# Per-head normalisation of the retention output: squares summed with tokens on partitions, factors spread on ScalarE and turned by four 128x128 transposes

## The chip, the cores and the metric

The kernel runs on one core of a Trainium2 chip. Its time is the device time of one execution in microseconds (us). Three executions of the kernel before took 1422.23, 1422.47 and 1424.04 us, with a median of 1422.47 us. A further execution was profiled; it took 1422.08 us. The profile names the engines PE (TensorE matmuls), PEld (TensorE weight loads), DVE (VectorE), ACT (ScalarE), POOL (GpSimd) and SP (SyncE, which issues the transfers here).

## The reference

Two layers of a hybrid backbone work on 1024 latent tokens and 256 context tokens of width 1024. In each layer one input projection feeds a short convolution, a two-directional retention with 6 heads of 64 channels, and a neighbourhood attention with 6 heads; each branch is gated, and one output projection with a LayerNorm closes the layer. The second layer needs no context output. The change concerns only the normalisation of the retention output, per token and head, over the head's 64 channels:

```
def head_norm(o):
    of = o.astype(F32)
    mu = jnp.mean(of, axis=-1, keepdims=True)
    var = jnp.mean(jnp.square(of - mu), axis=-1, keepdims=True)
    return (of - mu) * lax.rsqrt(var + LN_EPS)

y = from_heads(head_norm(o)) * jax.nn.silu(g)
```

In the kernel the mean is already removed when the values V are written (each head's V has its mean over channels subtracted), so what is left is a sum of squares, a reciprocal square root and a product.

## The kernel before, in words

Activations are kept transposed, channels on the 128 partitions and tokens along the free dimension. Tokens are cut in three groups: 512, 512 and 256 (context), numbered 0, 1 and 2. A projection unit (`proj_T`, lines 271 to 280) multiplies 128 columns of the weight with one token group in 24 matmuls: 8 chunks of the width, three products each of a high and a low part. Such matmuls, written to `ps_pj`, move 512 columns (256 for the context). `proj_V` (line 392) makes values with tokens on partitions: 24 matmuls of 256 columns for 128 tokens, in ten tiles. The weights come in 512-wide tiles through a ring of five (`wh`, the high part, cast on ACT at line 225; `wl`, the low part, subtracted on DVE or POOL at line 217). A value unit holds four of the five.

The six heads are three pairs p = 0, 1, 2; a pair fills 128 partitions. For each pair the program first runs the K, Q and V projections and then starts `core(p)` (line 420), a generator: it gives up control with `yield n` and is resumed when the recorded cost of the matmuls issued since has reached n. The next pair's projections (for p = 2 the gate projections of line 620) are issued meanwhile, so the yields set the PE order, which is taken as written. The other engines' orders come from a scheduler. Every engine works its own list in order.

Inside `core`, after the chunk states, each token group goes through `output` (lines 516 to 533: PE accumulates `ps_pv`, ACT copies it to `oT` and squares it into `ret_sq`), `scores` of the next group (PE, then DVE and POOL make `ret_s` and `ret_q`), and `norm` (lines 535 to 571). Layer 0 takes the groups in the order 2, 0, 1 for each pair, layer 1 takes 0 and 1: 9 and 6 norms, 15 in all, 12 of them of 512 tokens (four chunks of 128) and 3 of 256 (two chunks). The last norm of a pair is followed on PE by projection matmuls, the others by the next group's `output`.

The norm before has eight steps: a PE product of the 0/1 selector `selv` with the squares, chunk j on partitions 32j to 32j+31 (line 541); a 32x32-block transpose on DVE to `ct` (544); scale and add of epsilon to `c8` on POOL (546); the power -1/2 to `r8` on POOL (550); a split of the factor into a high and a low part, `rr`, in three DVE operations (554 to 556); after a yield, a PE transpose of `rr` (559) and a masked spread to `r16` on DVE (561); after another yield, one PE product with `sel16` that brings the factors to all channels (566); and the product with `oT` on DVE (569). The PSUM tag `pt` has two banks, and `norm` takes three in turn.

Of the kernel before, what the change touches and what calls it, by code (L numbers as in the profile page):

```python
# [10 lines left out]
F = mybir.dt.float32  # L11
R = mybir.dt.float32r
AF = mybir.ActivationFunctionType
ALU = mybir.AluOpType
# [6 lines left out]
HD = 64  # L21
ALPHA = (2 * DEPTH) ** 0.25
EPS = 1e-5
# [10 lines left out]
def f32(ap):  # L34
    return ap.bitcast(F)
# [43 lines left out]
def backbone(ctx: ExitStack, tc: tile.TileContext, io):  # L79
    nc = tc.nc  # L80
    pe, act, dve, pool, sp = nc.tensor, nc.scalar, nc.vector, nc.gpsimd, nc.sync
    od = Order()

    def mm(out, lhsT, rhs, start, stop, cost):
        pe.matmul(out, lhsT, rhs, start=start, stop=stop)  # L85
        od.t += cost
        od.poll()

    const = ctx.enter_context(tc.tile_pool(name="const", bufs=1))
# [5 lines left out]
    def bank(tag, bufs):  # L95
        return psum.tile([128, 512], F, tag=tag, bufs=bufs, name=f"ps_{tag}")
# [3 lines left out]
    ps_t = lambda: bank("pt", 2)  # L100
    ps_v = lambda: bank("pv", 1)

    def load_const(name, shape):
        t = const.tile(shape, F, name=f"c_{name}")
        sp.dma_start(t, io[name])
        return t
# [5 lines left out]
    mhalf = const.tile([128, 8], F, name="mhalf")  # L112
# [12 lines left out]
    def transpose(out, in_):  # L125
        pe.transpose(out, in_, ident[:in_.shape[0], :in_.shape[0]])  # L126
        od.t += 109
        od.poll()
# [124 lines left out]
    def new_h():  # L253
        return [[hpool.tile([128, KC, n], R, tag=f"h{j}{g}", name=f"h{j}{g}")
                 for j in range(2)] + [[]] for g, (o, n) in enumerate(GRP)]
# [7 lines left out]
    def accumulate(ps, w, h, g, kks):  # L263
        n = GRP[g][1]
        ready(h, g)
        for kk in kks:
            for i, (a, b) in enumerate(PASS):
                mm(ps[:, :n], w(kk, a), h[g][b][:, kk, :], kk == 0 and i == 0,
                   kk == KC - 1 and i == 2, n / 2.37)
# [113 lines left out]
    def retention(l, h, yT, vn, ctx_q, begin):  # L383
        groups = (0, 1, 2)
        qgroups = groups if ctx_q else (0, 1)
        with ExitStack() as st:
            rp = st.enter_context(tc.tile_pool(name=f"ret{l}", bufs=2, reuse_waits="tile"))
# [32 lines left out]
            def core(p, kT, qT, V, oT):  # L420
# [95 lines left out]
                def output(g, sq_in):  # L516
                    o, n = GRP[g]
                    ov = ps_v()
                    for j in range(n // 128):
                        c = o // 128 + j  # L520
                        for step in range(2):
                            for hh in range(2):
                                dst = ov[hh * 64:hh * 64 + 64, j * 128:(j + 1) * 128]
                                if step == 0:
                                    mm(dst, V[:, c, hh * HD:(hh + 1) * HD],
                                       sq_in[hh][0][:, j * 128:(j + 1) * 128], True, False, 141)
                                else:
                                    mm(dst, SS[:, c, hh * HD:(hh + 1) * HD],
                                       sq_in[hh][1][:, j * 128:(j + 1) * 128], False, True, 141)
                    act.copy(oT[:, o:o + n], ov[:, :n])  # L530
                    sq = t2("ret_sq")
                    act.activation(sq[:, :n], oT[:, o:o + n], AF.Square)
                    return sq

                def norm(g, sq):
                    o, n = GRP[g]
                    nch = n // 128
                    vps = ps_t()
                    np_ = 32 * nch
                    for j in range(nch):  # L540
                        mm(vps[32 * j:32 * j + 32, :128], selv, sq[:, j * 128:(j + 1) * 128],
                           True, True, 80)
                    ct = rp.tile([128, 128], F, tag="ct", bufs=1, name="ct")
                    dve.transpose(ct[:np_], vps[:np_, :128])
                    c8 = rp.tile([128, 4, 2], F, tag="c8", bufs=2, name="c8")
                    pool.tensor_scalar(
                        c8[:np_], ct[:np_].rearrange("p (b c) -> p b c", c=32)[:, :, 0:2],
                        1.0 / HD, EPS, ALU.mult, ALU.add)
                    r8 = rp.tile([128, 4, 2], F, tag="r8", bufs=2, name="r8")
                    pool.tensor_tensor(r8[:np_], c8[:np_], mhalf[:np_, 0:8].rearrange(  # L550
                        "p (b c) -> p b c", c=2), ALU.pow)
                    rr = rp.tile([128, 4, 2, 2], F, tag="rr", bufs=2, name="rr")
                    rh = rp.tile([128, 4, 2], R, tag="rh", bufs=2, name="rh")
                    dve.tensor_copy(rh[:np_], r8[:np_])
                    dve.tensor_copy(rr[:np_, :, 0, :], f32(rh[:np_]))
                    dve.tensor_tensor(rr[:np_, :, 1, :], r8[:np_], f32(rh[:np_]), ALU.subtract)
                    yield 6500
                    rt = ps_t()
                    transpose(rt[0:16, :np_], rr[:np_].rearrange("p b x h -> p (b x h)"))
                    r16 = rp.tile([16, 4, 128], R, tag="r16", bufs=1, name="r16")  # L560
                    dve.tensor_tensor(r16[:, :, :np_],
                                      rt[0:16, :np_].unsqueeze(1).to_broadcast([16, 4, np_]),
                                      mask16.unsqueeze(2).to_broadcast([16, 4, np_]), ALU.mult)
                    yield 2700
                    bc = ps_t()
                    mm(bc[:, :n].rearrange("p (b q) -> p b q", b=4), sel16,
                       r16[:, :, :np_], True, True, n / 2.37)
                    ov_v = oT[:, o:o + n].rearrange("p (g b t) -> p b g t", b=4, t=32)
                    dve.tensor_tensor(ov_v, ov_v,
                                      bc[:, :n].rearrange("p (b g t) -> p b g t", b=4, t=32),  # L570
                                      ALU.mult)

                order = ((2,) if ctx_q else ()) + (0, 1)
                sc = scores(order[0])
# [3 lines left out]
                for i, g in enumerate(order):  # L578
                    sq = output(g, sc)
                    yield 800  # L580
                    if i + 1 < len(order):
                        sc = scores(order[i + 1])
                    yield 800
                    yield from norm(g, sq)
                    done.append((p, g))

            tiles = []
            for p in range(3):
# [4 lines left out]
                    oT=rp.tile([128, TOK], F, tag="oT", bufs=3, name="oT")))  # L593
# [319 lines left out]
    h = new_h()  # L913
# [51 lines left out]
    def first_w(u):  # L965
        return lambda kk, i: wts[u][kk // 4][i][:, (kk % 4) * 128:(kk % 4 + 1) * 128]
# [5 lines left out]
    def begin_stage(i):  # L972
        kks = STAGES[i]
        tiles = stage_load(kks)
        if i == 0:
            small()
        stage_x(kks)
        if 0 in kks or 4 in kks:
            for u, c0 in enumerate((C_RK, C_RQ)):
                wts[u].append(w_half(0, c0, kks[-1] // 4))  # L980
        return od.start(stage(kks, tiles))

    begin_stage(0)
    for i, kks in enumerate(STAGES):
        if i + 1 < len(STAGES):
            begin_stage(i + 1)
        if i == 1:
            selv = load_const("selv", [128, 32])
            mask16 = load_const("mask16", [16, 4])
            sel16f = load_const("sel16", [16, 128])  # L990
            sel16 = const.tile([16, 128], R, name="sel16r")
            dve.tensor_copy(sel16, sel16f)
            rmask = load_const("rmask", [128, 16])
            cmask = load_const("cmask", [128, 24])
        for g in range(3):
            od.until(lambda: all((g, kk) in have for kk in kks))
            accumulate(acc_k[g], first_w(0), h, g, kks)
            if g < 2:
                accumulate(acc_q[g], first_w(1), h, g, kks)
# [26 lines left out]
    for l in range(DEPTH):  # L1026
# [12 lines left out]
        with ExitStack() as st:  # L1039
# [62 lines left out]
            for t in range(8 if last else 10):  # L1102
# [16 lines left out]
                for c in range(DM // w):  # L1119
                    hf, o = c * w // 512, c * w % 512  # L1120
# [32 lines left out]
            if not last:  # L1153
                h, mod = h_next, mod_n
# [88 lines left out]
```

## Time and profile before

| what | value |
|---|---|
| three executions, median | 1422.47 us |
| profiled execution, its own time | 1422.08 us |
| its span (first to last instruction) | 1420.3 us |
| granted TensorE clock over the span | 0.993 |
| busy: PE / DVE / ACT / POOL | 1371.0 / 959.7 / 469.0 / 330.1 us |
| norms, first and last `oT` product | 131.0 and 1029.4 us |

Times in the views are counted from the span's start. A row of the timeline gives the start, the time from the first start to the last end of what is merged in it, the engine, the line, the operation, the tiles written and read, the shapes and the count; in brackets stands the idle time before it and what ended it. Neighbouring matmuls overlap, so what a step on PE costs is read from starts, not from durations. An fp32 matmul leaves two records in the trace, a projection matmul one. A row of waits gives the total, the number and the longest.

### The profile page before, as it was taken

The numbers are of one execution on the slowest core, as the hardware profiler recorded it, in microseconds if no ns is written. First come the engines' busy times: TensorE is split into PE (matmuls) and PEld (weight loads), VectorE is DVE, ScalarE is ACT, GpSimd is POOL, SyncE is SP. The second block draws the span as 40 slices with busy tenths as digits, with TensorE's granted clock in tenths as the row PEclk, the third lists the DMA queues.
The fourth block names the chain that finished last, engine by engine and source line by source line (L and its number), as shares of the span: only waits on it lengthen the run. The fifth ranks groups of instructions, "written<-read, shape, count | busy, mean of one in ns | idle before, by whom it ended". The sixth has DMA issues, their size and how long they took to land.

```text
span 1420.3 us, 23906 instructions
## 1 busy us (share of the span) xinstructions
PE 1371.0 (97%) x9016; PEld 1156.0 (81%) x9016; DVE 959.7 (68%) x2392; ACT 469.0 (33%) x985; POOL 330.1 (23%) x281
## 2 busy tenths in 40 slices
PE   7999999999999999999999999999999999999997
PEld 4788878877888888878887798888777878787886
DVE  4677465648887886865887656565578756365686
ACT  3322121223452443443344322121234435354310
POOL 1405132342002203000344405050431031120121
PEclk9999999999999999999999999999999999999999
DMA  9720110224124224116443211111242220302642
GB/s 282 224 57 20 38 38 28 70 72 125 54 60 141 74 69 122 50 56 204 152 139 107 81 49 31 49 30 50 75 138 67 59 73 30 93 23 83 203 153 89
DMA packets 160852, 126.33 MB, mean 89 GB/s; under 512 B 10320, under 2 KB 146144, under 8 KB 160736
## 3 DMA queue, kind: packets, MB, share of 16 engines
q1 hardware_dynamic: 160736, 124.80, 28.8%
q8 instruction: 71, 1.16, 0.3%
q14 instruction: 45, 0.37, 0.1%
HBM read 103.01 MB, written 21.76 MB: 88 GB/s over the span
## 4 chain that ended last, share of the span: by engine, by line
PE 80%; DVE 9%; issue 2%; DMA 1%; POOL 1%; ACT 1%; SPq 0%; POOLq 0%; DVEq 0%; ACTq 0%
PE ps_pj L85 62%; PE ps_pv L85 6%; PE ps_pt L126 6%; PE ps_s L85 6%; DVE acc L197 1%; DVE rsw L379 1%; DMA E<-in_rpb 1%; PE ps_pt L85 1%; POOL B L711 1%; DVE P L692 1%; DVE ret_q L508 0%; DVE qd L487 0%; DVE wl L217 0%; DVE ret_s L499 0%; DVE sm L406 0%
## 5 line engine op out<-in xcount | busy, mean ns | idle before, releaser
L85 PE MATMUL ps_pj<-h,wh 128*128 128x512 f32 (+1 forms) x2128 | 622.8, 373 | 3.2 <-ACT wh L225 3.2
L85 PEld LDWEIGHTS ps_pj<-h,wh 128*128 128x128 f32 x2128 | 379.3, 189 | 67.0 <-issue 5.5
L85 PE MATMUL ps_pj<-h,wl 128*128 128x512 f32 (+1 forms) x1064 | 397.1, 373 | 0.0
L85 PEld LDWEIGHTS ps_pj<-h,wl 128*128 128x128 f32 x1064 | 201.4, 189 | 34.3 <-issue 4.0
L85 PE MATMUL ps_pj<-wo,yh 128*128 128x512 f32 (+1 forms) x608 | 181.7, 381 | 0.0
L85 PE MATMUL ps_pj<-wh,h 128*128 128x256 f32 x960 | 180.4, 288 | 0.7 <-ACT nv L412 0.7
L85 PEld LDWEIGHTS ps_pj<-wh,h 128*128 128x128 f32 x960 | 153.7, 196 | 2.8 <-issue 1.8
L217 POOL TENSOR_TENSOR wl<-wr,wh 128x512 fp32r<-128x512 f32 x32 | 43.8, 1369 | 461.0 <-ACT wh L225 386.3
L85 PE MATMUL ps_pj<-wl,h 128*128 128x256 f32 x480 | 138.2, 288 | 4.4 <-DVE wl L217 2.9
L85 PEld LDWEIGHTS ps_pj<-wo,yh 128*128 128x128 f32 x608 | 111.9, 188 | 21.2 <-issue 0.5
L85 PE MATMUL ps_pj<-wo,yl 128*128 128x512 f32 (+1 forms) x304 | 116.1, 382 | 0.0
L225 ACT CAST wh<-wr 128x512 fp32r<-128x512 f32 x128 | 79.2, 621 | 111.1 <-PE ps_pj L85 100.1
L197 DVE SCALAR_TENSOR_TENSOR acc<-wm,c_silu,acc 128x256 f32<-128x256 f32 x224 | 110.5, 534 | 5.7 <-DMA wm<-in_w_mod 5.2
L751 ACT ACTIVATE P<-P,nm 128x640 f32<-128x640 f32 (+1 forms) x96 | 77.2, 804 | 96.9 <-DVE nm L749 96.0
L85 PEld LDWEIGHTS ps_pj<-wl,h 128*128 128x128 f32 x480 | 94.0, 196 | 5.3 <-DVE wl L217 3.1
L761 ACT COPY PT<-ps_pt 128x512 f32<-128x512 f32 (+1 forms) x108 | 60.5, 560 | 87.9 <-PE ps_pt L126 87.0
L217 DVE TENSOR_TENSOR wl<-wr,wh 128x512 fp32r<-128x512 f32 x96 | 68.5, 716 | 29.1 <-ACT wh L225 27.0
L126 PE MATMUL ps_pt<-c_ident,P 128*128 128x128 f32 x480 | 73.1, 279 | 3.2 <-DVE P L692 2.9
L85 PE MATMUL ps_s<-KS,QH 128*128 128x256 f32 x204 | 59.7, 311 | 9.3 <-DVE mx L747 7.6
L85 PEld LDWEIGHTS ps_pj<-wo,yl 128*128 128x128 f32 x304 | 57.2, 188 | 10.8 <-issue 0.5
L126 PEld LDWEIGHTS ps_pt<-c_ident,P 128*128 128x128 f32 x480 | 54.5, 141 | 13.9 <-issue 7.4
L85 PE MATMUL ps_pv<-PT,VA 128*64 128x128 f32 x960 | 64.3, 278 | 0.0
(175 smaller groups left out, 1951.7 us busy)
## 6 DMA issues: line engine op xcount, KB each, us to landing
wr<-in_w_in SPq DMA_DIRECT2D x104, 256.0 KB
wm<-in_w_mod SPq DMA_DIRECT2D x128, 128.0 KB
wr<-yT SPq DMA_DIRECT2D x36, 256.0 KB
yT<-ystage SPq DMA_DIRECT2D x32, 256.0 KB
wr<-in_w_out SPq DMA_DIRECT2D x32, 256.0 KB
wm<-in_w_mod SPq DMA_DIRECT2D x12, 512.0 KB
wr<-in_w_in SPq DMA_DIRECT2D x48, 128.0 KB
z<-in_x SPq DMA_DIRECT2D x8, 512.0 KB
```

What stands on the lines that cost most here:

```text
L85: pe.matmul(out, lhsT, rhs, start=start, stop=stop)
L126: pe.transpose(out, in_, ident[:in_.shape[0], :in_.shape[0]])
L197: dve.scalar_tensor_tensor(acc[:, v], t, c, acc[:, v], ALU.mult, ALU.add)
L217: eng.tensor_tensor(lo, raw, f32(hi), ALU.subtract)
L225: act.copy(hi, raw)
L379: dve.tensor_tensor(sw, sw, rs[:, o:o + n], ALU.mult)
L692: dve.tensor_scalar(P[:, :n], P[:, :n], r, 0.5, ALU.mult, ALU.mult)
L711: pool.tensor_tensor(B, bass.AP(tensor=E.tensor, offset=E[:, o:o + 1].offset, ap=[list(E.ap[0]), [1, nc_], [RPB_W, 16]]), rmask.unsqueeze( ...
L751: act.activation(P[:, :256 + n], P[:, :256 + n], AF.Exp, bias=nm, accum_out=s)
L761: act.copy(PT[:, :n], pt[:, :n])
```

## The change

The squares become the stationary operand: for each chunk of 128 tokens PE multiplies the transposed squares by `selv`, now two columns wide, which leaves the two sums of a token on the token's partition. DVE scales them and adds epsilon straight from PSUM, POOL takes the power as before, ACT repeats each factor over 64 columns (`rb`, 128x512) with the scale 0.5, and after one yield PE transposes `rb` in four plain 128x128 transposes. DVE multiplies `oT` by the result. The DVE transpose, the high and low parts, the masked spread, the `sel16` product and the constants `mask16` and `sel16` go. One yield of 6000 stands where 6500 and 2700 stood.

```diff
@@ norm(g, sq)
                     vps = ps_t()
-                    np_ = 32 * nch
                     for j in range(nch):
-                        mm(vps[32 * j:32 * j + 32, :128], selv, sq[:, j * 128:(j + 1) * 128],
-                           True, True, 80)
-                    ct = rp.tile([128, 128], F, tag="ct", bufs=1, name="ct")
-                    dve.transpose(ct[:np_], vps[:np_, :128])
+                        mm(vps[:, 2 * j:2 * j + 2], sq[:, j * 128:(j + 1) * 128], selv,
+                           True, True, 220)
                     c8 = rp.tile([128, 4, 2], F, tag="c8", bufs=2, name="c8")
-                    pool.tensor_scalar(
-                        c8[:np_], ct[:np_].rearrange("p (b c) -> p b c", c=32)[:, :, 0:2],
-                        1.0 / HD, EPS, ALU.mult, ALU.add)
+                    dve.tensor_scalar(c8[:, :nch], vps[:, :2 * nch].rearrange(
+                        "p (b c) -> p b c", c=2), 1.0 / HD, EPS, ALU.mult, ALU.add)
                     r8 = rp.tile([128, 4, 2], F, tag="r8", bufs=2, name="r8")
-                    pool.tensor_tensor(r8[:np_], c8[:np_], mhalf[:np_, 0:8].rearrange(
-                        "p (b c) -> p b c", c=2), ALU.pow)
-                    rr = rp.tile([128, 4, 2, 2], F, tag="rr", bufs=2, name="rr")
-                    rh = rp.tile([128, 4, 2], R, tag="rh", bufs=2, name="rh")
-                    dve.tensor_copy(rh[:np_], r8[:np_])
-                    dve.tensor_copy(rr[:np_, :, 0, :], f32(rh[:np_]))
-                    dve.tensor_tensor(rr[:np_, :, 1, :], r8[:np_], f32(rh[:np_]), ALU.subtract)
-                    yield 6500
-                    rt = ps_t()
-                    transpose(rt[0:16, :np_], rr[:np_].rearrange("p b x h -> p (b x h)"))
-                    r16 = rp.tile([16, 4, 128], R, tag="r16", bufs=1, name="r16")
-                    dve.tensor_tensor(r16[:, :, :np_],
-                                      rt[0:16, :np_].unsqueeze(1).to_broadcast([16, 4, np_]),
-                                      mask16.unsqueeze(2).to_broadcast([16, 4, np_]), ALU.mult)
-                    yield 2700
+                    pool.tensor_tensor(r8[:, :nch], c8[:, :nch], mhalf.rearrange(
+                        "p (b c) -> p b c", c=2)[:, :nch], ALU.pow)
+                    rb = rp.tile([128, 512], F, tag="rb", bufs=1, name="rb")
+                    act.activation(rb[:, :n].rearrange("p (b c d) -> p b c d", c=2, d=HD),
+                                   r8[:, :nch].unsqueeze(3).to_broadcast([128, nch, 2, HD]),
+                                   AF.Copy, scale=0.5)
+                    yield 6000
                     bc = ps_t()
-                    mm(bc[:, :n].rearrange("p (b q) -> p b q", b=4), sel16,
-                       r16[:, :, :np_], True, True, n / 2.37)
-                    ov_v = oT[:, o:o + n].rearrange("p (g b t) -> p b g t", b=4, t=32)
-                    dve.tensor_tensor(ov_v, ov_v,
-                                      bc[:, :n].rearrange("p (b g t) -> p b g t", b=4, t=32),
-                                      ALU.mult)
+                    for j in range(nch):
+                        transpose(bc[:, j * 128:(j + 1) * 128], rb[:, j * 128:(j + 1) * 128])
+                    dve.tensor_tensor(oT[:, o:o + n], oT[:, o:o + n], bc[:, :n], ALU.mult)
@@ start of the program
         if i == 1:
-            selv = load_const("selv", [128, 32])
-            mask16 = load_const("mask16", [16, 4])
-            sel16f = load_const("sel16", [16, 128])
-            sel16 = const.tile([16, 128], R, name="sel16r")
-            dve.tensor_copy(sel16, sel16f)
+            selv = const.tile([128, 2], F, name="c_selv")
+            sp.dma_start(selv, io["selv"][:, 0:2])
```

The yields move work on every engine, inside the retention stages alone; outside them each engine's list is the same, but for the constants at the start. The first place is PE's list in the norm of the first pair's group 0 in layer 0. Here `h` and `wh`/`wl` with `ps_pj` are projection matmuls (with `wh,h` or `wl,h` they are value matmuls), and the row of `ps_pv` is the next group's `output`. Before:

```order
L85 MATMUL ps_pt<-ret_sq,c_selv 32x128 x4
...
L126 MATMUL ps_pt<-c_ident,rr 16x128
L85 MATMUL ps_pj<-wh,h_89 128x256
...
L85 MATMUL ps_pt<-r_1694,sel16r 128x512
L85 MATMUL ps_pv<-ret_s,V 64x128 x2
L85 MATMUL ps_pv<-ret_q,SS 64x128 x2
```

Now:

```order
L85 MATMUL ps_pt<-c_selv,ret_sq 128x2 x4
L85 MATMUL ps_pj<-h_91,wl 128x512
...
L126 MATMUL ps_pt<-c_ident,rb 128x128 x4
L85 MATMUL ps_pv<-ret_s,V 64x128 x2
L85 MATMUL ps_pv<-ret_q,SS 64x128 x2
```

Before, 60 matmuls of 256 columns stand between the sums and the transpose of `rr`, and 25 more ahead of the `sel16` product. Now 10 matmuls of 512 and 36 of 256 columns stand between the sums and the transposes of `rb`, and the next `output` follows at once.

The second place is DVE's list at the same norm. `L377`, `L379` and `L380` are the rotation of the next pair's queries, `L486` to `L508` belong to `scores`, `L217` is a weight's low part. Before:

```order
L377 STREAM_SHUFFLE rsw<-rraw 128x512
L486 COPY qd<-qT 64x512
L379 TENSOR_TENSOR rsw<-rsw,rs 128x512
L487 COPY qd<-qT 64x512
L380 TENSOR_TENSOR qT<-rraw,rsw 128x512
L499 TENSOR_TENSOR ret_s<-ps_s,D 128x512
L508 TENSOR_TENSOR ret_q<-qT,Wq 64x512
...
L508 TENSOR_TENSOR ret_q<-qd,Wq 64x512
L544 STREAM_TRANSPOSE ct<-ps_pt 128x128
```

Now (line 543 makes `c8`, line 556 is the product with `oT`, here of group 2):

```order
L556 TENSOR_TENSOR oT<-oT,ps_pt 128x256
L380 TENSOR_TENSOR qT<-rraw,rsw 128x512
L486 COPY qd<-qT 64x512
L487 COPY qd<-qT 64x512
L499 TENSOR_TENSOR ret_s<-ps_s,D 128x512
...
L508 TENSOR_TENSOR ret_q<-qd,Wq 64x512
L543 TENSOR_SCALAR c_1539<-ps_pt 128x8
L377 STREAM_SHUFFLE rsw<-rraw 128x512
L379 TENSOR_TENSOR rsw<-rsw,rs 128x512
```

The rotation of group 1's queries, which stood ahead of the scores and of the norm's first DVE step, now stands behind them.

The third place is ACT's list there, with the new `rb`:

```order
L549 ACTIVATE rb<-r_1439 128x256
L376 ACTIVATE rraw<-ps_pj 128x512
L530 COPY oT<-ps_pv 128x512
L532 ACTIVATE ret_sq<-oT 128x512
L549 ACTIVATE rb<-r_1541 128x512
L376 ACTIVATE rraw<-ps_pj 128x512
L225 CAST wh<-wr 128x512 x2
L373 ACTIVATE qT<-ps_pj 128x256
```

Before, the same rows stood without the two of `rb`, and nothing on ACT waited for POOL there. Now the queries' copy `rraw` and the two weight casts stand behind `rb` of group 0.

## The prediction

> **What bounds the kernel now.** I read the page first: busy time by engine, then the chain that ended last.
>
> ```profile
> span 1420.3 us, 23906 instructions
> ...
> PE 1371.0 (97%) x9016; PEld 1156.0 (81%) x9016; DVE 959.7 (68%) x2392; ACT 469.0 (33%) x985; POOL 330.1 (23%) x281
> ...
> PE 80%; DVE 9%; issue 2%; DMA 1%; POOL 1%; ACT 1%; SPq 0%; POOLq 0%; DVEq 0%; ACTq 0%
> ```
>
> PE is busy nearly throughout and carries 80% of the chain; DVE carries 9% of it, so a step on DVE counts only where PE waits for it. A change here is worth two things: what it adds to or takes from PE's own list, and which waits of PE it ends or makes. The second view is therefore PE's waits; two of its rows belong to the norm.
>
> ```profile
> PE ps_pt L126 <- DVE rr L556: 5.8, 2, 2.9
> ...
> PE ps_pt L85 <- DVE r L561: 0.8, 1, 0.8
> ```
>
> Two waits of 2.9 us stand before the transpose of `rr`, one of 0.8 us before the `sel16` product. The other twelve norms cost PE no wait. The third view is the timeline at the first long wait (first pair, group 0, layer 0), DVE's rows and then PE's.
>
> ```profile
> 134.74 0.73 DVE L377 STREAM_SHUFFLE rsw<-rraw 128x512 f32<-128x512 f32 x1
> ...
> 143.60 0.30 DVE L544 STREAM_TRANSPOSE ct<-ps_pt 128x128 f32<-128x128 f32 x1
> ...
> 146.59 0.16 DVE L556 TENSOR_TENSOR rr<-r,rh 128x8 f32<-128x8 f32 x1
> ```
>
> ```profile
> 136.15 0.43 PE L85 MATMUL ps_pt<-ret_sq,c_selv 128*32 128x128 f32 x8
> ...
> 143.61 0.28 PE L85 MATMUL ps_pj<-wl,h 128*128 128x256 f32 x1
> 146.90 0.37 PE L126 MATMUL ps_pt<-c_ident,rr 128*16 128x128 f32 x1 [2.89 <-DVE rr L556]
> ```
>
> PE had the sums ready at 136.58, but DVE reached them at 143.60: from 134.74 on it worked through the rotation of the next queries and the scores, which stand ahead in its list. From there to the end of `rr` it took 3.15 us. PE had run out of the matmuls that the first yield put in between and stood still. The second long wait has the same cause one pair later.
>
> **The change part by part. First, the two long waits.** DVE's list now has `c8` ahead of the rotation of group 1. The times below follow the new lists with today's durations:
>
> ```profile
> L550 POOL TENSOR_TENSOR r<-c,mhalf x15: 1629/1637/1652, 123.3 to 1021.4; 128x8 f32<-128x8 f32 x12, 64x8 f32<-64x8 f32 x3
> ```
>
> ```profile
> L376 ACT ACTIVATE rraw<-ps_pj 128x512 f32<-128x512 f32 x21 | 12.3, 595 | 52.0 <-PE ps_pj L85 51.9
> ```
>
> The norm of group 2 starts as before; its transposes come 28 instead of 31 projection steps later, and the next output follows without the second yield, so group 0's sums come some 4 us earlier, at about 131.8 to 132.5. DVE then still has the group's scores to finish; four operations that now take from 140.69 to 143.60, 2.9 us, start when PE's score products end, near 131, so `c8` comes at 134.0 to 134.6. With 0.2 us for it (an estimate: below `ct`'s 0.30), 1.64 for the power, 0.60 for `rb` (like the 128x512 copy of line 376) and 0.1 us a hop, `rb` stands at 137. PE's list holds 10 steps of 512 and 36 of 256 columns between: at 0.23 and 0.12 us, 6.6 us, so PE asks at about 139. Two us are left, and the wait falls away. Measured from 143.61 to 146.90 it is 3.29 us, of which 0.23 are the matmul and the transpose themselves: 3.06 us, twice: **-6.1 us**.
>
> The third wait stood in the last norm of layer 0, where the second yield found no projection left and the two products came one behind the other. Now 28 projection steps (6.4 us) stand between sums and transposes and DVE is nearly idle there: **-0.8 us**. The norms without a wait keep 6.4 to 6.6 us of cover for a chain of 0.2 + 1.64 + 0.60 + hops, 2.8 us, plus queueing. For it to show, queues must add 3.7 us.
>
> **Second, PE's own list.** Costs are read from starts, net of the projection step, which is 0.23 us. The sums before, in layer 1, four chunks:
>
> ```profile
> 1004.88 0.40 PE L85 MATMUL ps_pj<-h,wl 128*128 128x512 f32 x1
> 1005.21 0.42 PE L85 MATMUL ps_pt<-ret_sq,c_selv 128*32 128x128 f32 x8
> 1005.56 0.72 PE L85 MATMUL ps_pj<-h,wh 128*128 128x512 f32 x2
> 1006.12 0.40 PE L85 MATMUL ps_pj<-h,wl 128*128 128x512 f32 x1
> ...
> 1012.28 0.39 PE L85 MATMUL ps_pj<-h,wl 128*128 128x512 f32 x1
> 1012.51 0.39 PE L85 MATMUL ps_pj<-h,wh 128*128 128x512 f32 x1
> 1012.74 0.27 PE L126 MATMUL ps_pt<-c_ident,rr 128*16 128x128 f32 x1
> 1012.76 0.48 PE L85 MATMUL ps_pj<-h,wh 128*128 128x512 f32 x1
> 1013.08 0.40 PE L85 MATMUL ps_pj<-h,wl 128*128 128x512 f32 x1
> ...
> 1015.90 0.49 PE L85 MATMUL ps_pt<-r,sel16r 16*128 16x512 f32 x1
> 1016.32 0.44 PE L85 MATMUL ps_pv<-ret_s,V 128*64 128x128 f32 x4
> ...
> 1028.58 0.39 PE L85 MATMUL ps_pj<-h,wl 128*128 128x512 f32 x1
> 1028.90 0.49 PE L85 MATMUL ps_pt<-r,sel16r 16*128 16x512 f32 x1
> 1029.32 0.72 PE L85 MATMUL ps_pj<-h,wh 128*128 128x512 f32 x2
> 1029.88 0.40 PE L85 MATMUL ps_pj<-h,wl 128*128 128x512 f32 x1
> ```
>
> Sums: 1004.88 to 1006.12 is 1.24, less three steps (0.69): 0.55 us; two chunks I count alike, since the four run side by side on 32 columns each. Transpose of `rr`: 0.57 less 0.46, 0.11 us. `sel16` product: 1.30 less 0.69, 0.61 us ahead of projections, and 0.42 us from its start to the next ahead of an output; for two chunks half the columns, 0.31. Before, then, 1.27 us in a pair's last norm, 1.08 in another of four chunks, 0.97 with two.
>
> Of the new steps the trace has the transposes:
>
> ```profile
> 997.33 0.62 PE L85 MATMUL ps_pj<-h,wh 128*128 128x512 f32 x2
> 997.80 0.60 PE L126 MATMUL ps_pt<-c_ident,ST 128*128 128x128 f32 x4
> 998.15 0.48 PE L85 MATMUL ps_pj<-h,wl 128*128 128x512 f32 x1
> 998.46 0.63 PE L85 MATMUL ps_pj<-h,wh 128*128 128x512 f32 x2
> ```
>
> 1.13 less 0.69: 0.44 us for four, 0.11 each. The new sums aren't in the trace: per chunk two records, each with a weight tile of 128x128 fp32 and two moving columns. Bounds are records with 128-column weights:
>
> ```profile
> 1002.97 1.16 PE L85 MATMUL ps_s<-qT,kT 64*128 64x128 f32 x16
> 1004.06 0.50 PE L85 MATMUL ps_pj<-h,wl 128*128 128x512 f32 x1
> ```
>
> ```profile
> L126 PEld LDWEIGHTS ps_pt<-c_ident,P 128*128 128x128 f32 x480 | 54.5, 141 | 13.9 <-issue 7.4 <-DVE P L692 3.4 <-DVE nm L749 0.6
> ```
>
> The scores, with weights on 64 rows, take 1.09 us for 16, 0.068 each; a weight load of the transposes by itself lasts 0.141. I take the transposes' own spacing, 0.11, the only one with a full 128x128 tile: 0.88 us for four chunks, 0.44 for two. Now 0.88 + 0.44 = 1.32 us, and 0.66 with two chunks. Against before: +0.05 in six norms (0.3), +0.24 in six (1.4), -0.31 in three (-0.9): **+0.8 us**, between -3.7 (108 records at 0.068) and +4.1 (at 0.141).
>
> What picks between these rows also stands in the Trainium skill, TensorE: Matmul & The Clock Gate, section "LDWEIGHTS (loading the stationary operand)": a load takes the number of columns over 1.2 GHz and the rows don't matter, which is 107 ns for 128 columns and 27 for the 32 that the selector had. By that rule the sums get dearer, as by the transposes' row; by the scores' row they would cost the same as today. The transposes' 0.11 agrees with it, while the scores' 0.068 is below it, and the measured row that fits the new shape is kept.
>
> **Third, the rest.** DVE sheds five operations of a four-chunk norm and gains `c8`; ACT gains 0.60 us per norm, POOL sheds `c8`'s. None is on PE's path where PE doesn't wait, so they count nothing, unless ACT comes late (below). At the start two transfers go, on a queue that the first weights share:
>
> ```profile
> 30.05 0.43 SPq L105 DMA_DIRECT2D c_mask<-in_mask  x1
> 30.53 0.41 SPq L105 DMA_DIRECT2D c_sel<-in_sel  x1
> ```
>
> That could bring the next loads forward by 0.84 us at most; I count 0, the cautious end. Outside the retention stages the lists are unchanged, so what is won there shifts all that follows.
>
> **Sum.** 1422.08 - 6.1 - 0.8 + 0.8 = 1416.0 for the profiled execution. The median lies 0.4 above that execution, so the forecast is 1416.4 us.
>
> **The rivals.** *The waits stay* (1422.5 us). If `c8` still starts 7 us after the sums, as `ct` did at 143.60, then the chain ends 7.0 + 2.8 us after them, 3.2 past PE's 6.6: both long waits stay, the tail's 0.8 pays for PE's 0.8. For it speaks that DVE works its list in order and is crowded there; against it, that the rotation now stands behind `c8`. It also covers the case that the waits only shift to `ret_s`.
>
> *ACT is held up* (the slower one). `rb` waits on POOL, and ACT's next rows wait with it: the queries' copy and the cast of the value unit's last weight quarter, on whose low part PE waits. That quarter has no slack today:
>
> ```profile
> 136.14 0.62 ACT L225 CAST wh<-wr 128x512 fp32r<-128x512 f32 x1 [1.44 <-PE ps_pj L85]
> ...
> 138.87 1.36 POOL L217 TENSOR_TENSOR wl<-wr,wh 128x512 fp32r<-128x512 f32 x1
> ...
> 140.32 0.34 PE L85 MATMUL ps_pj<-wl,h 128*128 128x256 f32 x1
> ```
>
> POOL ends at 140.23, PE uses it at 140.32. After the change the cast ends near 138.2 (`rb` at 137, the copy 0.6, the cast 0.6), POOL first finishes the rotation (about 139.9) and then this part, 141.3. PE comes later too: value matmuls start at 137.6, twelve of them, the transposes 0.44 and the output's 32 records (2.2, an estimate at the scores' 0.068) stand ahead, and it asks at 142.3. One us is left. This place comes four times (two pairs, two layers; in layer 1 I get 0.7). Every further us costs up to 4 us. The kernel is slower by over 2.8 us from (6.1 + 2.8) / 4 + 0.9 = 3.1 us of lateness on; at 3.5 us it takes 1416.4 + 4 x 2.6 = 1426.8 us. The Trainium skill, the same page's table at its head, calls the queues of ScalarE, VectorE and GpSimdE strictly first in, first out; the lists and waits here agree.
>
> *Weight loads dearer or cheaper*: 1419.7 at 0.141 us a record, 1411.9 at 0.068. These stay on the faster side and make the forecast's own range.
>
> **How the numbers follow.** Forecast with its range of load costs 0.77; the waits stay 0.14; ACT held up 0.09, of which 0.02 end within 2.8 us of today's time. What a measurement of this kernel can tell from no change is 0.2%, 2.8 us: faster means below 1419.6, slower above 1425.3. The first case is faster but for its last tenth of a us; the second is the same; the third is split. So faster 0.77, the same 0.16, slower 0.07. The range reaches from the cheap loads, 1411.9, to the dear ones with a us or so of lateness, 1421.0, which leaves out most of the two rivals.
>
> **What the profile afterwards would show.** No wait of PE for `rb` and none on a weight's low part at the value units bear out the first part; a row of PE waiting for ACT `rb`, or for POOL or DVE `wl` near 142 and 884, speaks for a rival. Eight records of the sums filling about 0.88 us and four transposes 0.44 bear out the second; 0.5 or 1.1 us for the sums moves the time by 4 us. The forecast is wrong if the group 0 `c8` starts later than 136 or if waits appear in the second layer, where there are none of the norm today.

## The result, and the profile after

| | kernel before | changed kernel |
|---|---|---|
| median of five executions | 1422.63 us | 1410.83 us (1408.68 to 1412.18) |
| ratio | | 0.9911, 95% interval 0.9897 to 0.9926 |
| profiled execution, its span | 1422.08, 1420.3 us | 1410.83, 1409.0 us |

The change is worth 11.8 us of the medians, about twice the 6.1 us forecast, and the time lies 1.1 us below the predicted range. Run once more beside other kernels, the changed kernel gave a ratio of 0.9904 (0.9888 to 0.9920).

The page of the changed kernel, with busy time by engine and the chain that ended last:

```profile
span 1409.0 us, 23900 instructions
...
PE 1367.4 (97%) x9040; PEld 1165.1 (83%) x9040; DVE 940.6 (67%) x2331; ACT 478.1 (34%) x1000; POOL 320.8 (23%) x266
...
PE 82%; DVE 9%; DMA 3%; issue 2%; ACT 1%; POOL 1%; SPq 1%; POOLq 0%; DVEq 0%; ACTq 0%
```

PE is busy 3.6 us less than before (1371.0 us) although it has 24 records more. So it did not only stop waiting: some of its work went faster. That is the first sign of what the forecast lacked.

The waits of PE in the changed kernel; no row for `rr`, `r` or `rb` is among them:

```profile
PE ps_s L85 <- DVE mx L732: 7.4, 8, 1.8
PE ps_pv L85 <- DMA wm<-in_w_mod: 7.1, 4, 4.7
...
PE ps_pj L85 <- DVE wl L217: 3.0, 1, 3.0
...
PE ps_pj L85 <- ACT nv L412: 1.3, 1, 1.3
...
PE ps_pj L85 <- POOL wl L217: 0.2, 1, 0.2
```

DVE at the place of the first long wait (first pair, group 0, layer 0):

```profile
130.94 0.67 DVE L508 TENSOR_TENSOR ret_q<-qd,Wq 64x512 f32<-64x512 f32 x1
131.54 0.15 DVE L543 TENSOR_SCALAR c<-ps_pt 128x8 f32<-128x8 f32 x1
134.68 0.01 DVE L377 LOAD_MASK_SELECT rsw<-rraw  x1 [2.98 <-ACT rraw L376]
```

The squares' sums are read at 131.54, ahead of the rotation, which starts 3.1 us later. Before, the rotation came first.

**Where the time went.** Both kernels issue the same 5544 matmuls into the projection banks, in the same order, so their start times can be compared one by one. The difference after minus before grows as follows (steps counted from 0):

| stretch | change, us | forecast |
|---|---|---|
| start, to step 170 (76.14 and 73.55) | -2.6 | 0 |
| norms of the first pair, layer 0 (to step 654) | -4.6 | -3.1 |
| norms of the second pair (to step 1038) | -4.35 | -3.1 |
| norms of the third pair, with the tail (to step 1320) | -1.1 | -0.8 |
| the rest of layer 0 | -0.6 | 0 |
| start of layer 1 (to step 3160) | +1.1 | 0 |
| norms of layer 1 (to step 4368) | +0.5 | +0.9 |
| to the end | +0.2 | 0 |

The sum is -11.4 us. Two things are missing from the forecast: 2.6 us at the start, and about 1.4 us behind each of the two long waits. The other rows nearly cancel; the +1.1 us at the start of layer 1 was not there in run 10, which won 1.7 us from step 1320 to step 3160 (the last section says why this differs).

**Behind the long wait** PE worked at half clock. Windows over the kernel before; the columns are busy time and records of PE, PEld, DVE, ACT and POOL, then the granted clock of PE, DMA share and GB/s:

```profile
143.00:146.90 3.90, 1.01 (x9) 0.84 (x8) 2.03 (x8) 0.00 (x0) 2.13 (x2) 0.99 0.24 70
146.90:150.30 3.40, 3.40 (x17) 3.40 (x18) 1.67 (x7) 0.53 (x2) 0.00 (x0) 0.51 0.05 13
150.30:153.70 3.40, 3.40 (x44) 3.00 (x43) 1.35 (x4) 0.27 (x1) 0.00 (x0) 1.00 0.09 26
```

After the idle of 2.89 us the clock stands at 0.51 for 3.4 us and then at 1.00. The matmuls show it directly, first right behind the stall, then 3.4 us later:

```profile
147.28 0.41 PE L85 MATMUL ps_pj<-wl,h 128*128 128x256 f32 x1
147.50 0.63 PE L85 MATMUL ps_pj<-wh,h 128*128 128x256 f32 x2
147.92 0.41 PE L85 MATMUL ps_pj<-wl,h 128*128 128x256 f32 x1
...
150.73 0.28 PE L85 MATMUL ps_pj<-wl,h 128*128 128x256 f32 x1
150.84 0.40 PE L85 MATMUL ps_pj<-wh,h 128*128 128x256 f32 x2
151.08 0.28 PE L85 MATMUL ps_pj<-wl,h 128*128 128x256 f32 x1
```

Three matmuls take 0.64 us at the first place (147.28 to 147.92) and 0.35 at the second. The changed kernel has 1.00 at that time, and no half clock from 30 us on until 341 us:

```profile
147.00:150.30 3.30, 3.30 (x30) 3.30 (x29) 1.44 (x4) 0.27 (x1) 0.00 (x0) 1.00 0.09 25
```

**At the start** two things change. PE's two waits for `wm`, which stood in the kernel before, are gone, and 1.9 us are won between step 30 and step 40:

```profile
41.19 0.64 PE L85 MATMUL ps_pv<-wm,c_silu 128*32 128x256 f32 x8 [0.60 <-DMA wm<-in_w_mod]
42.66 0.64 PE L85 MATMUL ps_pv<-wm,c_silu 128*32 128x256 f32 x8 [0.84 <-DMA wm<-in_w_mod]
```

And the rope tables (`rc`, `rs`) leave SP 2.6 and 2.1 us earlier. SP's queue before, then after:

```profile
57.69 0.34 SPq L596 DMA_DIRECT2D rc<-in_ropec  x1
58.15 0.36 SPq L597 DMA_DIRECT2D rs<-in_ropes  x1
```

```profile
55.06 0.51 SPq L581 DMA_DIRECT2D rc<-in_ropec  x1
56.06 0.34 SPq L582 DMA_DIRECT2D rs<-in_ropes  x1
```

POOL multiplies by them, and behind that in its list stands the low part of the first value weights, on which PE waits. POOL's first multiplication before, then after:

```profile
62.06 4.69 POOL L378 TENSOR_TENSOR rraw<-rraw,rc 128x512 f32<-128x512 f32 x3 [1.49 <-DVE rsw L377]
```

```profile
59.26 4.27 POOL L378 TENSOR_TENSOR rraw<-rraw,rc 128x512 f32<-128x512 f32 x3 [0.61 <-DVE rsw L377]
```

Both rows name DVE's shuffle, but the first shuffle ended 1.24 us ahead of POOL's start in the kernel before, and 0.35 us ahead in the changed one. That POOL waited for the tables in that time is inferred; run 3 has a row that names them. PE's wait for the low part before, and the same matmul after:

```profile
68.47 0.39 PE L85 MATMUL ps_pj<-wl,h 128*128 128x256 f32 x1 [1.50 <-POOL wl L217]
```

```profile
65.28 0.39 PE L85 MATMUL ps_pj<-wl,h 128*128 128x256 f32 x1 [0.22 <-POOL wl L217]
```

At this matmul 3.2 us are won; 0.6 are lost again by step 170, behind a new wait of 1.32 us for `nv`.

### The profile page after: what moved, and what is told of

Same layout as the page of the kernel before. It is cut to its first block, busy times and chain, and to the rows that moved or that the text cites. A ratio compares the mean times of both kernels' runs of the same rounds, so it can differ in the third digit from the quotient of the medians.

```text
span 1409.0 us, 23900 instructions
## 1 busy us (share of the span) xinstructions
PE 1367.4 (97%) x9040; PEld 1165.1 (83%) x9040; DVE 940.6 (67%) x2331; ACT 478.1 (34%) x1000; POOL 320.8 (23%) x266
## 4 chain that ended last, share of the span: by engine, by line
PE 82%; DVE 9%; DMA 3%; issue 2%; ACT 1%; POOL 1%; SPq 1%; POOLq 0%; DVEq 0%; ACTq 0%
PE ps_pj L85 62%; PE ps_pt L126 7%; PE ps_pv L85 7%; PE ps_s L85 6%; DVE acc L197 2%; DVE rsw L379 1%; DMA wm<-in_w_mod 1%; PE ps_pt L85 1%; DMA wr<-in_w_out 1%; DVE P L677 1%; DMA E<-in_rpb 1%; POOL B L696 1%; DVE wl L217 1%; DMA wr<-in_w_in 0%; DVE P L732 0%
## 5 line engine op out<-in xcount | busy, mean ns | idle before, releaser
L217 POOL TENSOR_TENSOR wl<-wr,wh 128x512 fp32r<-128x512 f32 x32 | 43.6, 1362 | 476.1 <-ACT wh L225 398.2
L217 DVE TENSOR_TENSOR wl<-wr,wh 128x512 fp32r<-128x512 f32 x96 | 69.7, 730 | 40.3 <-ACT wh L225 39.0
L404 DVE TENSOR_REDUCE sm<-ps_pj 128x2 f32<-128x128 f32 x60 | 17.4, 290 | 79.9 <-PE ps_pj L85 79.4
```

The costliest lines, as they stand in the source:

```text
L217: eng.tensor_tensor(lo, raw, f32(hi), ALU.subtract)
L404: dve.tensor_reduce(sm, ps[:, :128].rearrange("p (h d) -> p h d", d=HD), AX.X, ALU.add)
```

## The experiments

Two theories were formed on the missing 5 us. **C**: a long idle of PE costs its length and then about 1.5 us more, at half clock. **S**: the two loads that the change removes (`mask16`, `sel16`) held the start back. The rivals: a wait costs its length alone (**L**), and the loads are worth their own issue time at most. The kernel before took 1420.6, 1420.75 and 1422.35 us beside the three groups of runs; ratios are to it.

**1. The old norm with its transpose later.** Nothing of the change but the end of the two long waits:

```diff
-                    yield 6500
+                    yield 6500 + (3500 if ctx_q and p < 2 and g == 0 else 0)
```

> The kernel before, with only the transpose of `rr` put 3500 cost units (about 3.8 us of projection matmuls) later in the two norms where PE stood still (layer 0, first and second pair, group 0); the norm's operations and the start are as before. Both theories say that the two idle stretches of 2.9 us go. Theory C (clock): an idle of 2.9 us also halves the granted clock for some 3 us behind it, about 1.5 us lost each time, so 2 x (3.06 + 1.5) = 9.1 us are won: 1413.5 us, and the 3 us behind the two places show a clock of 1.00 instead of 0.50. Rival L (length): a stall costs its length, 6.1 us are won: 1416.5 us, and the other 5 us of the change came from elsewhere.

Measured: 1413.89 us, ratio 0.9948 (0.9930 to 0.9966), 7.4 us faster with 4.8 to 9.9 as the interval. It holds both forecasts. The place itself says more. The idles are gone, the clock there is 1.00, and in the first pair 3.3 us are won (from step 438 to step 686), after a new wait has been paid:

```profile
147.63 0.38 PE L85 MATMUL ps_pj<-wh,h 128*128 128x256 f32 x1 [1.02 <-ACT nv L412]
```

So 4.3 us were won there before that wait, where L has 3.06 to give. In the second pair it is 3.0 us and the same new wait of 1.0, 4.0 together.

**2. The same by 2000 units**, which leaves a part of the idle.

> As the run with 3500, but 2000 units (about 2.2 us) later: the two idles shrink from 2.9 to about 0.7 us and stay. Theory C: an idle of 0.7 us leaves the clock at 1.00 (the trace before has idles of 1.2 and 1.5 us with 1.00 behind them), so 2 x (2.2 + 1.5) = 7.4 us are won: 1415.2 us. Rival L: 2 x 2.2 = 4.4 us: 1418.2 us.

Measured: 1416.49 us, ratio 0.9965 (0.9952 to 0.9978), 5.0 us faster with 3.1 to 6.8 as the interval; that is nearer to L's 4.4 than to C's 7.4. An idle of 0.61 us stays, with a clock of 1.00 behind it. C's 7.4 lies outside the interval, L's 4.4 inside it. Locally 3.3 and 3.1 us are won in the two pairs, for idles that shrank by 2.3 each: 0.8 to 1.0 us each beyond L, and less than the 1.5 that C counts. The profiled execution, one of the slower ones (1418.83 us), also had 6.8 us of half clock at 805 and again at 1061, where the kernel before had 3.4 each. The places speak against L, and C's price for a wait was too high here.

**3. The two loads in a later stage of the start**, in the kernel before:

```diff
         if i == 1:
             selv = load_const("selv", [128, 32])
-            mask16 = load_const("mask16", [16, 4])
-            sel16f = load_const("sel16", [16, 128])
-            ...
+        if i == len(STAGES) - 1:
+            mask16 = load_const("mask16", [16, 4])
+            sel16f = load_const("sel16", [16, 128])
+            ...
```

> The kernel before, with only the loads of `mask16` and `sel16` and the cast of `sel16` moved from the second start stage to the last one, so that they no longer stand ahead of the third stage's weights on SP's queue; norm and waits as before. Theory S (start): the two short transfers hold the weights of the third and fourth stage back, PE's two waits for `wm` at 41.2 and 42.7 (0.60 and 0.84 us) go with the lag that follows, 2.6 us won: 1420.0 us. Rival: they are worth at most their own issue time, 0.84 us: 1421.8 us or more, and the 2.6 us of the changed kernel's start were chance of one profile.

Measured: 1423.75 us, ratio 1.0020 (1.0007 to 1.0032): slower, against both. PE's waits for `wm` near 42 us went as S said. But the loads now stood closer ahead of the rope tables, which left SP at 58.60, and POOL waited for them:

```profile
63.61 4.70 POOL L378 TENSOR_TENSOR rraw<-rraw,rc 128x512 f32<-128x512 f32 x3 [4.00 <-DMA rs<-in_ropes]
```

PE then waited 4.1 instead of 1.5 us for POOL's `wl`, with a stretch of half clock behind. S named only the first of two waits: the 1.9 us that go with the waits for `wm` are won up to step 40 here too, but PE then stands at the later wait, which hangs on the rope tables, so that they are lost again.

**4. The changed kernel with the two loads put back**, unused:

```diff
             sp.dma_start(selv, io["selv"][:, 0:2])
+            mask16 = load_const("mask16", [16, 4])
+            sel16f = load_const("sel16", [16, 128])
+            sel16 = const.tile([16, 128], R, name="sel16r")
+            dve.tensor_copy(sel16, sel16f)
```

> The changed kernel, with only the two loads and the cast put back where they were (unused there). Theory S: 2.6 us lost of 1410.8: 1413.4 us, and PE waits for `wm` near 41 us come back. Rival: at most 0.84 us lost: 1411.7 us.

Measured: 1412.71 us, ratio 0.9935 (0.9922 to 0.9949), against 0.9911 without them: 3.4 us lost; the two ratios come from different groups of runs, and their intervals overlap by 0.0004. Against the 0.9904 of run 10 it is 4.4 us, without overlap. PE's wait for POOL's `wl` is back with 1.8 us.

**5. The kernel before without the two loads**: memsets on POOL stand in their place, so the factors' values are not computed.

> The kernel before with the loads of `mask16` and `sel16` left out: two memsets on POOL at the start stand in their place, so the factors' values are not computed; cast, norm and waits as before. The run with the loads moved to the last start stage came out 2.8 us slower than before: PE's waits for `wm` near 42 us went, but the two loads then stood ahead of the rope tables on SP's queue, POOL multiplied by them later, and PE waited 4.1 instead of 1.5 us for the first value weight's low part that stands behind on POOL. Theory S2: what counts is the time at which SP issues the rope tables (57.7 us before, 55.1 in the changed kernel), so without the two loads they come about 2.5 us earlier and 2.6 us are won: 1420.0 us. Rival: the loads hold nothing back beyond their own 0.84 us: 1421.8 us or more.

Measured: 1419.56 us, ratio 0.9986 (0.9974 to 0.9999), 2.0 us faster. S2's 2.6 us and the rival's 0.84 both lie in the interval. In the trace the rope tables leave SP at 55.83, and step 115 comes at 65.83, 2.6 us earlier. Over all traces the start sorts by the loads: step 170 comes at 76.14, 75.88 and 76.74 us in the three kernels with the loads in their old place and the old norm, at 78.53 in run 4, and between 73.41 and 75.29, 74.2 on average, in the six without the loads and with the start otherwise unaltered. The loads are worth about 2 us, with a spread of up to 1.9 us between the executions of one sort.

**6. The changed kernel asks earlier.**

```diff
-                    yield 6000
+                    yield 2000
```

> The changed kernel with the yield between sums and transposes cut from 6000 to 2000 units, so PE asks for `rb` about 4.3 us earlier in all 15 norms. In the trace of the changed kernel `rb` is ready 1.4 to 4.1 us before PE asks; with 4.3 us less PE stands still 0.2 to 2.9 us at each, 22.8 us in all, seven of them for 1.9 us or more. Rival L (an idle costs its length): 1410.8 + 22.8 = 1433.6 us. Theory C (an idle of about 2 us and more is mostly followed by a stretch of 3 us or more at half clock, about 1.5 us lost each): five to seven such stretches, 7.5 to 10.5 us more: 1441 to 1444 us, and windows with a granted clock of 0.50 behind the longer idles, none behind those under 1 us.

Measured: 1439.16 us, ratio 1.0131 (1.0113 to 1.0150). L's time is excluded. C's is missed by 2 us, though as a ratio to the kernel before (1.0129 to 1.0150) it holds; that is in part luck, since neither the waits nor the number of stretches came out as counted. PE waited 19.0 us for `rb`, less than the 22.8 expected, so L would have 1429.8. Three of the longer idles in the norms were followed by half clock, others were not:

```profile
123.23:126.60 3.37, 3.37 (x30) 3.12 (x32) 1.26 (x3) 0.00 (x0) 0.00 (x0) 0.53 0.25 72
281.44:284.80 3.36, 3.36 (x40) 2.76 (x40) 0.42 (x1) 0.93 (x2) 0.00 (x0) 1.00 0.31 93
```

The idle ahead of the first was 2.00 us, ahead of the second 2.53. In the profiled execution 27.0 us more than the changed kernel's were 19.0 of waits, some 5 of half clock (three stretches of 3.4 us) and 1 of a later start; 2 us stay without a row. The medians differ by more, 31 us by the two ratios, and no profile shows that rest.

**7. A yield of 4000.** Meant as the case of short idles only.

> The changed kernel with the yield cut from 6000 to 4000 units: PE asks for `rb` about 2.15 us earlier, and by the lead that `rb` has in the trace (1.4 to 4.1 us) stands still 0.2 to 0.7 us in six of the 15 norms, 2.2 us in all. Theory C and rival L both say 2.2 us more than the changed kernel, 1413.0 us: idles this short leave the clock alone. A third possibility, that short idles halve the clock too: six stretches of 1.5 us, 1422 us.

Measured: 1425.11 us, ratio 1.0017 (1.0007 to 1.0027): 15.7 us slower than the changed kernel beside it, and slower than the kernel before. All three forecasts missed. The idles were not short. PE's wait, and DVE ahead of it:

```profile
PE ps_pt L126 <- ACT rb L549: 9.4, 5, 4.3
```

```profile
130.28 1.68 DVE L380 TENSOR_TENSOR qT<-rraw,rsw 128x512 f32<-128x512 f32 x1
131.88 0.68 DVE L499 TENSOR_TENSOR ret_s<-ps_s,D 128x512 f32<-128x512 f32 x1
132.48 0.67 DVE L508 TENSOR_TENSOR ret_q<-qT,Wq 64x512 f32<-64x512 f32 x1
133.08 0.67 DVE L499 TENSOR_TENSOR ret_s<-ps_s,D 128x512 f32<-128x512 f32 x1
133.68 0.67 DVE L508 TENSOR_TENSOR ret_q<-qd,Wq 64x512 f32<-64x512 f32 x1
134.28 0.15 DVE L543 TENSOR_SCALAR c<-ps_pt 128x8 f32<-128x8 f32 x1
```

With this yield the sums and scores fall at another place among the projections, and DVE's list has the rotation ahead of `c8` again, as in the kernel before. The sums were ready at 128.15 and read 6.1 us later; PE stood still for 4.33 us, and in the second pair for 4.31. Behind the first:

```profile
136.90:140.00 3.10, 3.06 (x24) 2.73 (x26) 0.69 (x1) 0.00 (x0) 0.00 (x0) 0.51 0.00 0
```

The two pairs lost 6.8 and 6.7 us, some 2.4 each beyond the idle. This is the prediction's rival "the waits stay", made by one number: with the new norm in place, the order alone decides between 1409 and 1425 us. The case of short idles was not tried by this run.

**8. The first value weights ahead of the rotation**, in layer 1. The one long wait left in that layer, 3.0 us at 799, has 6.8 us at half clock behind it. Windows of the changed kernel:

```profile
796.20:799.20 3.00, 0.01 (x1) 0.00 (x0) 3.00 (x4) 0.00 (x0) 2.33 (x2) 0.86 0.00 0
799.20:802.60 3.40, 3.40 (x16) 3.40 (x17) 2.23 (x11) 0.21 (x1) 0.00 (x0) 0.50 0.74 215
802.60:806.00 3.40, 3.40 (x21) 3.40 (x21) 2.67 (x16) 1.51 (x7) 0.00 (x0) 0.62 0.12 36
```

```diff
                 if p == 0:
                     begin(k_ev, q_ev)
+                    w = None if later is None else w_pair(l, C_RV, C_NV)
+                    for rotate in later or ():
+                        rotate()
                     dec = decay_tables(l, rp)
-                    proj_V(p, T["V"])
+                    proj_V(p, T["V"], w)
```

Here `begin` issues the copies out of PSUM alone and keeps the rotations in `later`.

> The changed kernel, and in layer 1 alone the casts and low parts of the first value weights are put ahead of the rotation of the keys and queries on DVE and POOL (the copies out of PSUM stay first). In the changed kernel PE waits there 3.0 us for a weight's low part at 799.2, and runs at half clock for 6 us behind it. Theory C: the wait goes and with it the half-clock stretch, 1.5 to 3 us: 1410.8 - 3.0 - 1.5 to 3.0 = 1404.8 to 1406.3 us. Rival L: 1407.8 us. Second rival: PE waits in its place for the cast or the copies on ACT, and under 1 us is won: 1410 us or more.

Measured: 1408.60 us, ratio 0.9916 (0.9900 to 0.9933), no gain over the changed kernel's 0.9911 or 0.9904. The second rival has it: PE got its weights and then stood still three value tiles later, since DVE's list had the rotations ahead of those tiles' own operations.

```profile
804.33 0.38 PE L85 MATMUL ps_pj<-wh,h 128*128 128x256 f32 x1 [2.21 <-ACT nv L420]
```

**9. The rotations handed out between the value tiles**, one behind each of the first four, and the decay tables behind all, in both layers:

```diff
+                    w = w_pair(l, C_RV, C_NV)
+                    proj_V(p, T["V"], w, later)
-                    dec = decay_tables(l, rp)
-                    proj_V(p, T["V"])
+                    dec = decay_tables(l, rp)
```

`proj_V` takes one rotation out of `later` behind each value tile.

> The changed kernel with the first pair's rotations of keys and queries handed out one behind each of the first four value tiles, the first value weights' casts ahead of them and the decay tables behind all, in both layers; the work is the same. The run that only put the weights ahead ended the wait of 3.0 us at 799 but found one of 2.2 us four tiles later, for the value tile's operations that stood behind the rotations. If that order was the cause, both waits fall under 1 us in layer 1: by theory C 3.0 us and 1.5 to 3 us of half clock are won, 1404.8 to 1406.3 us; by rival L 1407.8 us. If DVE's and POOL's work there is simply too much for the time, a wait of 2 us stays somewhere: 1409 us or more.

Measured: 1405.69 us, ratio 0.9882 (0.9867 to 0.9898). Beside it the changed kernel took 1409.43 us; the lead is 3.7 us, with the ends of the two intervals overlapping. The wait of 3.0 us is gone, 0.8 us are left at 801, and no half clock stands behind. So the order was the cause of the wait. Between C and L the total doesn't decide: the time lies in C's range, but the lead over the changed kernel beside it lies between L's 3.0 us and C's 4.5 to 6. This is the fastest kernel of the study.

**10. The changed kernel once more.**

> The changed kernel once more, unaltered, beside the two runs below on one chip. If the start's gain is owed to the two loads and not to chance, its profile has again no wait of PE for POOL's `wl` above 0.5 us and the rope tables issued near 55 us; the ratio to the kernel before is again 0.990 to 0.993 (1408.5 to 1412.5 us where the kernel before takes 1422.6). By theory C its time follows the number of half-clock stretches, about 1.5 us each, of which two or three are to be seen behind the idles at 341 and 799.

Measured: 1409.43 us, ratio 0.9904 (0.9888 to 0.9920). The rope tables left SP at 56.55, PE's wait for POOL's `wl` was 0.5 us; the tables came 1.5 us later than in the first profile. Half clock stood behind the idle at 799.79 for 3.4 us this time, not 6.8, and not at all behind the one at 341, which lasted 1.72 us instead of 2.67; a stretch of 3.4 us at 1056 was new.

## Why the prediction was wrong, point by point

**The way was right.** The reads of the sums were forecast at 134.0 to 134.6, and came at 131.54; with the start's 2.6 us added, 134.1. `rb` was forecast for 137 and stood at 134.15 (136.75 on the same scale); PE asked 2.62 us later, where two were forecast. The tail wait went, and no wait for `rb` or for a value unit's last weights appeared in either layer. For the rival that ACT is held up, the terms named for PE add up to 141.7 us and not to 142.3; the rest must be value matmuls behind the output, which that list leaves out. POOL's part ended at 138.53 and PE used it at 140.13: 1.6 us were left, one was forecast.

**PE's own list was right.** The new sums and transposes of a norm in layer 1:

```profile
1005.20 0.39 PE L85 MATMUL ps_pj<-h,wl 128*128 128x512 f32 x1
1005.42 0.95 PE L85 MATMUL ps_pt<-c_selv,ret_sq 128*128 128x2 f32 x8
1006.23 0.72 PE L85 MATMUL ps_pj<-h,wh 128*128 128x512 f32 x2
1006.79 0.40 PE L85 MATMUL ps_pj<-h,wl 128*128 128x512 f32 x1
...
1012.50 0.39 PE L85 MATMUL ps_pj<-h,wh 128*128 128x512 f32 x1
1012.73 0.60 PE L126 MATMUL ps_pt<-c_ident,rb 128*128 128x128 f32 x4
1013.08 0.47 PE L85 MATMUL ps_pj<-h,wh 128*128 128x512 f32 x1
1013.39 0.39 PE L85 MATMUL ps_pj<-h,wl 128*128 128x512 f32 x1
```

1.59 less three steps of 0.23 is 0.90 us for the eight sums (forecast 0.88), 0.89 less two steps is 0.43 for the four transposes (0.44). The row of the transposes was the right one to price a weight tile of 128 columns; the scores' 0.068 us would have given 0.54.

**The step that failed first** is "3.06 us, twice: -6.1 us". It counted the wait from its last matmul ahead to the first behind and took PE to be at its usual pace from there on. The third view showed a matmul of 256 columns in 0.28 us ahead of the stall and stopped at the stall's end; the rows right behind it, at 0.41, say otherwise. With them each wait was worth 4.35 to 4.6 us, not 3.06, so the two made -9.0 us. That the half clock belongs to the idle is shown by runs 1 and 7: without the idle the clock there is 1.00, and where an idle was made again by order alone, half clock came back with it.

The Trainium skill, TensorE: Matmul & The Clock Gate, section "Part 1: The HAM clock gate (the "warmup" mystery)", has the rule: PE's clock has two states, it falls to half after at least one idle window of about 3.4 us and comes back after a busy one, and the window runs freely. The traces agree on the two states, on the length, 3.4 us or twice that, and on windows that run freely: the stretches of a trace start on one grid of 3.413 us (last section). They differ on the idle: 1.9 us or more within one window brought half clock in 36 of 36 cases.

**The step that failed second** is "I count 0, the cautious end" for the two transfers less. The bound of 0.84 us was the issue time of the two alone. In the profile the rope tables behind them leave SP 2.6 and 2.1 us earlier and PE gains 2.6 us; over all traces it is about 2 (runs 3 to 5). That step looked at the first weights on that queue and not for what PE waits for last in the start, POOL's low part behind the rope tables, though the row of that wait, 1.5 us, was in the view of PE's waits. Why two issues of 0.4 us bring the tables forward by more than their own time isn't settled: other issues in that stretch last much longer than theirs (four for `wm` at 40.10 took 5.05 us before), and no run took them apart.

**The range** went down to 1411.9 us for cheap weight loads alone. It had no case in which a wait costs more than its length, nor one in which the start gains more than 0.84 us.

## What to carry to other kernels

A wait of the matmul engine of some 2 us or more is priced with what follows it: look at the granted clock and at the spacing of the matmuls in the 3.5 us behind it, and count the difference in. A single profile shows only how that wait fell in one execution. A load that goes from a shared queue is priced by what stands behind it on that queue and by the last wait that hangs on it, not by its own issue. Where a scheduler orders an engine's list, a number that moves one step may put it behind another stage's work: the same norm took 1409 us with a yield of 6000 and 1425 with 4000.

## What the runs showed of the hardware

In the twelve traces of this case (before, after and the ten runs), the granted clock, read in windows of 0.25 us, is at half in stretches of 3.4 us or of 6.8 and at 1.00 otherwise. This holds from 30 us after the start to 12 us before the end. Sorted by the idle of PE ahead (rows of 0.45 us and more):

| idle of PE, us | cases | half clock within 3.5 us |
|---|---|---|
| 2.8 to 4.4 | 20 | 18 |
| 1.7 to 2.8 | 34 | 19 |
| 0.45 to 1.7 | 164 | 11 |

All eleven of the last row lie within 4 us of another idle, such as 0.94 and 0.83 us around 42 us in run 4. A single idle below 1.7 us was never followed by half clock. The same idle in the same kernel came out differently in two executions: behind the one of 3.0 us at 799 stood 6.8 us of half clock in one profile of the changed kernel, 3.4 in the other, and none behind the same idle in run 1.

What decides is how the idle falls on a grid. The stretches of one trace start whole multiples of 3.413 us apart, to within 2 ns over as much as 1362 us (the stretch at the program's end is taken in), and the grid lies elsewhere in each execution. With the twelve traces cut into windows of their grids (those at full clock, from 26 us after the start to 16 us before the end) and PE's idle time added up in each:

| idle of PE in one window, us | windows | half clock in the next |
|---|---|---|
| 1.9 or more | 36 | 36 |
| 1.6 to 1.9 | 11 | 3 |
| less than 1.6 | 4740 | 0 |

So an idle of 2.9 us mostly brings a stretch, unless a line of the grid cuts it into two short parts, as it cut the one of 2.97 us in run 1 into 1.5 and 1.4; and the 0.94 and 0.83 us of run 4 fell into one window. Where a window at half clock was followed by another, PE had been idle in it for 0.6 to 1.1 us (4 cases); where full clock came back, for 0.8 us at most, mostly for none (39 cases). Each stretch of 3.4 us costs up to 1.7, so executions of one kernel differ by such steps. In the kernel before, five stretches make 17 us at half clock ahead of the end, in the changed kernel 10.2: the difference is worth up to 3.4 us, near the 2.8 that the two places give by themselves.
